# Left operands at fixed products in the pair stage and the way up, the last differences and the scan's later loads moved

## The chip, the cores and the metric

One core of one Trainium2 chip runs the whole program. The metric is device time in microseconds (us): the median of the runs of one kernel. The kernel before took 2461.01 us in the median of three runs (2454.09, 2461.01, 2461.89). The engines are TensorE (PE, the matmuls), VectorE (DVE), ScalarE (ACT), GpSimd (POOL) and SyncE (SP, which issues most DMA transfers). Each engine works through its own list of instructions in a fixed order.

## What is computed

One layer of a streaming encoder on 1088 tokens (1024 of a new stream, 64 of a running one), width 1024, all in fp32. Cut to what matters:

```
xn = rmsnorm(x);  z, xbc, dt, q, k, v, g_ssm, g_att = split(xn @ w_in)
y  = scan(silu(conv4(xbc)), softplus(dt), state)      # 32 heads in 4 groups
y  = rmsnorm(y * silu(z))
o  = attention(rope(rmsnorm(q)), rope(rmsnorm(k)) + cached keys, v)   # softmax - lam * softmax
x += (sig(g_ssm) * (y @ w_bs) + sig(g_att) * (o @ w_ba)) @ w_out
ha, hb = split(rmsnorm(x) @ w_up);  x += (silu(conv3(ha)) * hb) @ w_down
```

The outputs are the new x, the keys and values, the states of the scan and the last rows of both convolutions.

## The kernel before

**Products.** An fp32 operand is split in two parts that TensorE takes at full rate: hi, a cast by ACT, and lo, the difference from hi, made by DVE (`split`, L412). One product is then three matmuls of 128x128 by 128x272. Three stretches of the program multiply 2x2 blocks with seven block products instead of eight (a Strassen-Winograd scheme): the projections to q, k and z (16 pairs of output tiles in the list `INPUT`, called here the **pair stage**), the FFN's first matrix (22 pairs, the **way up**) and its second (12 pairs, the **way down**).

**A pair** has 7 products p0 to p6 in two halves s (columns), so 14 steps of 12 matmuls, in the order p0 s0, p0 s1, p1 s0 and so on. Step number = 2p+s. Accumulator banks and readers (`in_pair`, L574 on; the way up has the same in `pair`): p0 goes to bank a and ACT copies it to u1 (L622); p1 goes to b and DVE adds u1, giving u2 (L624); p2 goes on in a; p3 goes on in b, and DVE adds it to u1 (L626); p4 is in bank c and p5 in bank d, both read by DVE (L634); p6 goes on in bank c. So p6 of a half can't start until DVE has read p4 of that half; three steps (36 matmuls) lie between the end of p4 s0 and the start of p6 s0.

**Left operands.** Each pair has seven, built from four weight blocks q11, q12, q21, q22 that two loads `w_f` bring: q11, s2 = q21+q22-q11, q12, q11-q21, s1 = q21+q22, q22, and q12-s2. The sums are four operations on POOL (for pairs 0 and 1 on DVE), then each is split into hi and lo. Operands 0 to 3 go to four `wh` buffers, 4 to 6 to the two buffers of `w_hi` and `w_lo`. In the pair stage and on the way up a generator (`left_parts`, L495) yields the next pair's operands one by one; `more_left` (L539) takes one after each second step (s = 1), so all seven are made during the pair ahead. In the pair stage the lo part lags: `split_left` (L480) notes it and `low_left` (L488) writes it at the next call, behind DVE's last read. On the way down, the code already has a table (`down_left`, `lefts_at`): loads at step 4, operands 0 to 3 of the next pair at steps 8, 10, 11, 13, and operands 4, 5, 6 of a pair at steps 0, 1, 3 of that pair itself.

**Beside the pairs** of the pair stage runs side work, one unit per step (`take_turn`): step sizes, cached keys, and after the q and k pairs the finishing of q and k: POOL fetches a half row from the scratch `q_r` or `k_r` into a ring of four buffers `fx`, DVE scales it (L760 with the norm), ACT casts the hi part, SP stores it to `q_st` or `k_st`, DVE makes the rest (L717) and SP stores that. `done` (L601) squares a finished tile on ACT, DVE sums the squares (L614), and SP stores the tile. Rows live in two pools, `rows_l` and `rows_r`, which are opened where earlier pools (`xn`, `rr` on one side, `raw`, `st` on the other) have been released, so their first use waits for the last readers of those.

**The scan's start.** While the last attention and gate tiles run, `scan` fetches its first inputs: two spans of `in` (three loads each, L1170, L1171), three steps of `bc` (L1183), two `zin` (L1176). SP also issues the stores of the gate tiles, `g_sc<-gt` (L884), whose three `gt` buffers ACT fills from the banks (L881), and of the attention's output, `o_sc<-oh`, `o_sc<-ol` (L1103).

**The start of the way down.** It multiplies differences of rows that the way up has stored: `differences_of` (L1600 on) loads two rows `ht`, does four subtractions on DVE (L1607 to L1610) and stores to `t_sc`. A couple of rows is done at step 6 of the second pair after its last row was made; the last two couples come after pairs 1 and 2 of the way down. Right operands n and m are loaded, then split in place by L413 (ACT) and L414 (DVE).

**What sets the order.** The Tile framework schedules the program once, by a modelled timeline, priorities and the pins `issue_after` (this instruction not ahead of that one on its engine); the lists that result are fixed. So a move in the code moves neighbours too.

Of the kernel before, what the change touches and what calls it, by code (L numbers as in the profile page):

```python
# [62 lines left out]
IN_ROWS = dict(fs=2, fu=2, fp=3, fc=3, fx=4, ss=2)  # L63
# [27 lines left out]
def hybrid_layer(ctx: ExitStack, tc: tile.TileContext, xT, xt, prm, cst, rope, wvd, win, wbs, wba, wout, wup, wdn,  # L91
# [378 lines left out]
    def row(tag, name, dt=F32):  # L470
        if tag == "fa":
            return rows_l.tile([P, KT * P], dt, name=name, tag=tag, bufs=4)
        w = {"ss": T, "fs": 4 * P}.get(tag, HT)
        return rows_r.tile([P, w], dt, name=name, tag=tag, bufs=IN_ROWS[tag])

    def couple(t, n=2):
        return t[:, : n * QW].rearrange("p (a t) -> p a t", a=n)

    low, lagging = [], [True]

    def split_left(hi, lo, src):
        S.copy(hi, src)  # L482
        if lagging[0] and "read" in seen:
            low.append((hi, lo, src))
        else:
            V.tensor_tensor(out=lo, in0=src, in1=hi, op=ALU.subtract)  # L486

    def low_left():  # L488
        if low:
            with tc.issue_after(seen["read"].ins):  # L490
                for hi, lo, src in low:
                    V.tensor_tensor(out=lo, in0=src, in1=hi, op=ALU.subtract)
            low.clear()

    def left_parts(blocks, early=None, by=G, order=(0, 1, 2, 3)):  # L495
# [12 lines left out]
        def own(src):  # L508
            t = row("fa", "wh", R32)
            hi, lo = t[:, :n], t[:, 4 * P : 4 * P + n]  # L510
            split_left(hi, lo, src)
            return hi, lo

        def shared():
            t = [wp.tile([P, wide], R32, name=x, tag=x, bufs=2) for x in ("w_hi", "w_lo")]
            for i, src in enumerate((s1, q22)):
                hi, lo = (x[:, 512 * i : 512 * i + n] for x in t)
                split_left(hi, lo, src)
# [17 lines left out]
        split_left(hi, lo, s2)  # L536
        yield 6, (hi, lo)

    def more_left(f):  # L539
        low_left()  # L540
        x = next(coming, None)
        if x is not None:
            left.setdefault(f, {})[x[0]] = x[1]

# [21 lines left out]
    def split_part(n, *behind):  # L566
        with ExitStack() as pins:
            for x in behind:
                pins.enter_context(tc.issue_after(x.ins))
            for s in range(2):  # L570
                hi, lo = parts[n, s]
                split(hi, lo, lo.bitcast(F32))

    def in_pair(n):  # L574
# [43 lines left out]
        for _ in range(14):  # L618
# [8 lines left out]
            else:  # L627
# [7 lines left out]
                if s == 1:  # L635
                    done(r, c)
# [98 lines left out]
    def finishing(kind):  # L735
# [3 lines left out]
        for _ in range(4):  # L739
            yield  # L740
# [86 lines left out]
    coming = in_parts(1, early[1])  # L827
# [8 lines left out]
    for p, s in rest:  # L836
        pairs[0].send((p, s))
        if s == 1:
            more_left(1)
            if p in LATER:  # L840
                split_part(LATER[p], seen["copy"], seen["read"])
    while len(left[1]) < 7:
        more_left(1)
    beside = chain(one_by_one(steps()), cached_keys())
    for n in range(1, len(INPUT)):
        coming = in_parts(n + 1) if n + 1 < len(INPUT) else iter(())
        u = pairs[1] if n == 1 else begun_in(n)
        for at, (p, s) in enumerate(rest if n == 1 else [(p, s) for p in range(7) for s in range(2)]):
            u.send((p, s))
            if s == 1:  # L850
                more_left(n + 1)
# [4 lines left out]
        while n + 1 < len(INPUT) and len(left[n + 1]) < 7:  # L856
            more_left(n + 1)
        low_left()
        del left[n]
        if n == Q_DONE:  # L860
            beside = chain(beside, finishing("q"), finishing("k"))
    while take_turn(0):
        for _ in range(2):
            take_turn(1)
    lagging[0] = False
# [78 lines left out]
    with (tc.tile_pool(name="ak", bufs=1) as ak, tc.tile_pool(name="at", bufs=1) as at,  # L944
# [131 lines left out]
        def head_out(h, o_t, ssq, s0):  # L1076
# [15 lines left out]
            for b0 in range(0, 9, 4):  # L1092
# [9 lines left out]
                for u, t in enumerate((hi, lo)):  # L1102
                    load(out=o_sc[D * u + P * h : D * u + P * (h + 1), b0 * P : b0 * P + w], in_=t.bitcast(F32))  # L1103
# [60 lines left out]
    with (tc.tile_pool(name="sin", bufs=1) as sin, tc.tile_pool(name="sp", bufs=1) as sp,  # L1164
# [112 lines left out]
        def scan():  # L1277
            spans = [(g, c, w) for g in range(4) for c, w in WIDE]
            steps = [(i, g, c, w, o) for i, (g, c, w) in enumerate(spans) for o in range(0, w, P)]
            got, due = [fetch(*x) for x in spans[:2]], None  # L1280
            asked = [ask(*x) for x in steps[:3]]
            gates = [fetch_z(*x) for x in spans[:2]]
# [225 lines left out]

    ffn_o = tri[:, : 4 * FT].rearrange("p (f c) -> p f c", c=4)
# [144 lines left out]
    made = {}  # L1654

    def down_left(i, what):

        g, m = divmod(i, 4)
        n = P * (DOWN[g] // 2)
        if what == "load":  # L1660
            q = []
            for r in (m, m + 4):
                o = 1024 * first[g] + 2 * n * r
                w = wp.tile([P, wide], F32, name="w_f", tag="w_f", bufs=2)
                load(out=w[:, : 2 * n], in_=wdn[:, o : o + 2 * n])
                q += [w[:, :n], w[:, n : 2 * n]]
            q11, q12, q21, q22 = q
# [263 lines left out]
```

## Time and profile before

| | |
|---|---|
| median of 3 runs | 2461.01 us (2454.09 to 2461.89) |
| the profiled execution | 2447.27 us, of which the span is 2445.5 us |
| PE busy | 2394.9 us, 98% of the span, 18744 matmuls |
| DVE, ACT, POOL busy | 71%, 50%, 28% |
| granted TensorE clock | 0.995 in the mean |

The profiled execution is one run, 13.7 us under the median of the other three. Stretches by the place of the lines in the span: values 0 to 115 us, pair stage 115 to 483, attention 483 to about 1085, scan 1085 to about 1500, branches and output 1500 to 1720, way up 1720 to about 2195, way down about 2195 to 2436. A matmul's row gives about 290 ns but one starts about every 125 ns, since they overlap; a gap between matmuls is idle time of PE, and rows of waits name what ended it. Instructions of DVE also overlap a little (0.43 us each, one every 0.35).

### The profile page before, as it was taken

Reading aid. Unit: us, or ns where it says so; the run is one execution under the profiler, and the core shown is the slowest. Engines: PE = TensorE matmul, PEld = TensorE weight load, DVE = VectorE, ACT = ScalarE, POOL = GpSimd, SP = SyncE. Lnnn points to the kernel's source line nnn. Section 1 sums busy time; section 2 is a strip of 40 time slices with the busy share of each in tenths; the row PEclk is TensorE's granted clock in tenths of the full one; section 3 lists DMA queues with packets and bytes.
Section 4 is the critical chain, followed back from the end, with each engine's and each line's share of the span. In section 5 each row is a group of like instructions: output and inputs, shape, how many; then the busy total and the mean of one; then the engine's idle time right before and its main releaser. Section 6 shows DMA issues by size and latency. Waiting matters only on the chain.

```text
span 2445.5 us, 49342 instructions
## 1 busy us (share of the span) xinstructions
PE 2394.9 (98%) x18744; PEld 2319.6 (95%) x18744; DVE 1744.6 (71%) x3118; ACT 1224.1 (50%) x2707; POOL 689.0 (28%) x753
## 2 busy tenths in 40 slices
PE   8999999999999999999999999999999999999998
PEld 8999989999999999998899999999999999999998
DVE  4586867668687786865787665756977777777765
ACT  7354464356565665647665554434543343352442
POOL 0023333201011010104443331013255555534444
PEclk9999999999999999999999999999999999999999
DMA  7855758665445344345897954764123423467876
GB/s 245 283 177 184 241 184 317 219 192 154 152 151 161 123 148 134 114 154 176 270 332 257 339 176 149 218 205 150 58 90 145 154 80 142 150 212 214 220 177 105
DMA packets 283088, 449.79 MB, mean 184 GB/s; under 512 B 35609, under 2 KB 189346, under 8 KB 282850
## 3 DMA queue, kind: packets, MB, share of 16 engines
q1 hardware_dynamic: 271810, 420.30, 51.8%
q0 software_dynamic: 11040, 26.34, 5.4%
q8 instruction: 147, 2.41, 0.4%
q14 instruction: 91, 0.75, 0.1%
HBM read 294.03 MB, written 152.50 MB: 183 GB/s over the span
## 4 chain that ended last, share of the span: by engine, by line
PE 66%; DMA 7%; DVE 7%; issue 3%; POOL 2%; ACT 1%; SPq 0%; POOLq 0%; DVEq 0%; ACTq 0%
PE mx L1528 9%; PE mm L162 9%; PE mm L164 9%; PE mm L163 9%; PE mm L1528 4%; PE mx L1748 4%; PE po L1071 3%; PE mx L164 2%; PE mx L162 2%; PE mx L163 2%; PE mm L1748 2%; PE mx L587 2%; PE sc L1023 2%; PE sc L1022 2%; PE pt L1051 1%
## 5 line engine op out<-in xcount | busy, mean ns | idle before, releaser
L162 PE MATMUL mm<-b,w_hi 128*128 128x272 f32 x1792 | 529.0, 295 | 0.8 <-DVE b_g L230 0.7
L164 PE MATMUL mm<-b,w_lo 128*128 128x272 f32 x1792 | 522.7, 292 | 1.8 <-DVE w_lo L156 1.8
L163 PE MATMUL mm<-b,w_hi 128*128 128x272 f32 x1792 | 520.8, 291 | 0.0
L162 PEld LDWEIGHTS mm<-b,w_hi 128*128 128x128 f32 x1792 | 337.6, 188 | 7.3 <-issue 3.8
L163 PEld LDWEIGHTS mm<-b,w_hi 128*128 128x128 f32 x1792 | 337.8, 189 | 3.3 <-issue 2.6
L164 PEld LDWEIGHTS mm<-b,w_lo 128*128 128x128 f32 x1792 | 337.1, 188 | 3.7 <-DVE w_lo L156 2.4
L912 DVE SCALAR_TENSOR_TENSOR cc<-pre,par,cc 128x272 f32<-128x272 f32 (+1 forms) x288 | 140.1, 490 | 16.4 <-ACT cc L910 13.6
L1528 PE MATMUL mx<-m,w_hi 128*128 128x272 f32 x760 | 146.1, 289 | 1.3 <-ACT m L413 1.3
L1528 PE MATMUL mx<-n,wh 128*128 128x272 f32 x1080 | 144.3, 288 | 1.9 <-DVE u L1555 1.0
L1528 PEld LDWEIGHTS mx<-n,wh 128*128 128x128 f32 x1080 | 138.5, 188 | 2.5 <-DVE u L1555 1.2
L900 POOL COPY pre<-pre 128x3 f32<-128x3 f32 x72 | 22.4, 312 | 418.3 <-DVE cc L914 186.2
L1036 ACT ACTIVATE p_t<-sc,mx 128x512 f32<-128x512 f32 (+6 forms) x144 | 106.1, 739 | 63.4 <-DVE mx L1027 30.9
L156 DVE TENSOR_TENSOR w_lo<-w_f,w_hi 128x1024 fp32r<-128x1024 f32 (+1 forms) x82 | 103.7, 1266 | 46.2 <-ACT w_hi L155 43.5
L155 ACT CAST w_hi<-w_f 128x1024 fp32r<-128x1024 f32 (+1 forms) x82 | 85.9, 1048 | 70.2 <-PE mm L163 43.0
L1528 PEld LDWEIGHTS mx<-m,w_hi 128*128 128x128 f32 x760 | 119.3, 188 | 1.5 <-ACT m L413 1.5
L1545 POOL TENSOR_TENSOR hb<-hb,cc 128x544 f32<-128x544 f32 (+2 forms) x63 | 81.8, 1312 | 101.8 <-DVE hb L1566 50.6
L482 ACT CAST w_hi<-ws 128x512 fp32r<-128x512 f32 x76 | 46.9, 617 | 126.5 <-PE mx L1528 75.0
L1528 PE MATMUL mx<-m,w_lo 128*128 128x272 f32 x380 | 109.7, 289 | 0.0
L1208 ACT ACTIVATE bc<-bc,nacum 128x128 f32<-128x128 f32 (+1 forms) x288 | 87.2, 384 | 16.1 <-POOL bc L1206 15.7
L505 POOL TENSOR_TENSOR ws<-w_f 128x512 f32<-128x512 f32 x34 | 48.5, 1425 | 154.1 <-DMA w_f<-in_win_dram 64.7
L486 DVE TENSOR_TENSOR wh<-w_f,wh 128x512 fp32r<-128x512 f32 x65 | 66.7, 1028 | 26.9 <-ACT wh L482 26.9
L1430 POOL TENSOR_TENSOR s<-s,sq 128x272 f32<-128x272 f32 x24 | 30.5, 1271 | 192.9 <-DMA out_dram<-x 131.2
(467 smaller groups left out, 7093.2 us busy)
## 6 DMA issues: line engine op xcount, KB each, us to landing
w_f<-in_win_dram SPq DMA_DIRECT2D x78, 512.0 KB, 4.2
w_f<-in_wup_dram SPq DMA_DIRECT2D x45, 512.0 KB, 3.4
bc<-a_sc SPq DMA_DIRECT2D x32, 512.0 KB, 5.9
h_sc<-hb SPq DMA_DIRECT2D x44, 272.0 KB, 2.1
ht<-h_sc SPq DMA_DIRECT2D x22, 544.0 KB, 4.8
t_sc<-ht SPq DMA_DIRECT2D x22, 544.0 KB, 2.7
out_dram<-yq POOLq DMA_DIRECT2D x44, 272.0 KB, 5.2
x_sc<-cc SPq DMA_DIRECT2D x72, 136.0 KB, 2.4
```

What stands on the lines that cost most here:

```text
L155: S.copy(hi, w)
L156: V.tensor_tensor(out=lo, in0=w, in1=hi, op=ALU.subtract)
L162: PE.matmul(ps, a_hi, b_hi, start=i == 0, stop=False)
L163: PE.matmul(ps, a_hi, b_lo, start=False, stop=False)
L164: PE.matmul(ps, a_lo, b_hi, start=False, stop=i == n - 1)
L912: V.scalar_tensor_tensor(cc[:, :m], pre[:, i : i + m], cw(i), cc[:, :m], ALU.mult, ALU.add)
L1036: act(p_t[:n, :nk], sc[c][:n, :nk], AF.Exp, bias=mx[:n, c : c + 1], accum_out=dst)
L1071: PE.matmul(po[:n, :P], a_t[b // 4][:kw, b % 4 * P : b % 4 * P + n], rhs, start=b == 0, stop=b == nb - 1)
L1208: act(bc[:L, e, :L], bc[:L, e, :L], AF.Exp, bias=nacum[:L, ch, 8 * g + e : 8 * g + e + 1])
L1528: PE.matmul(ps, w[x][:, c], b[y][:, k], start=start and k == i == 0, stop=k == 3 and i == 2, skip_group_check=not start)
L1545: (V if f + 1 == FT else G).tensor_tensor(out=hb[h][:, o : o + n], in0=hb[h][:, o : o + n], in1=cc[:, d : d + n], op=ALU.mult)
L1748: PE.matmul(ps, w[y][:, c], b[z][:, k], start=start and k == j == 0, stop=k == n - 1 and j == 2, skip_group_check=not start)
```

## The change

- **Left operands.** The generator and the lagging lo parts go (`split_left`, `low_left`). The way down's table becomes general (`make_left`, `lefts_at`) and serves the pair stage and the way up too: loads at step 4, operands 0 to 3 of the next pair at steps 8, 10, 11, 13, operands 4, 5, 6 at steps 0, 1, 3 of the pair itself, each pinned behind the newest copy (ACT) and read (DVE). Pairs 1 and 2 of the pair stage and pair 1 of the way up, which begin with fewer steps, have tables of their own. The four sums of pair 1 of the pair stage move from DVE to POOL. The last sum is written over q12 instead of s2.
- **Rows.** The buffers `fs` (sums) and `fu` (u1, u2) move from pool `rows_r` to `rows_l`, so they lie over other earlier pools.
- **Squares and stores.** `done` is put off by one step (`ripe`), and the finishing of q and k starts one turn later (5 for 4).
- **Scan.** Only the first span and the first `bc` are loaded ahead; the second span, two `bc` and both `zin` come after the last store to `o_sc`.
- **Differences.** The third last couple moves from step 6 of the last pair of the way up to the end of pair 0 of the way down.

Line numbers after the change, for those below: L624 becomes L662, L626 L664, L634 L672, L614 L652, L760 L798, L717 L755; splits of left operands (L482, L486, L492) become L413, L414; L884 becomes L923, L1103 L1142, L1170 L1209, L1171 L1210, L1176 L1215, L1183 L1222, L1607 to L1610 L1650 to L1653, L1753, L1758, L1760, L1762 L1746, L1751, L1753, L1755.

The order of the lists shows it in three places. First DVE in the pair stage, pair 7 of the pairs (the last of k), from the second read of p1 to the reads of p4 (L634). `wh<-` and `w_lo<-` are lo parts of left operands, `x` are rows of the finishing, `ss` the sum of squares. Before:

```order
L624 TENSOR_TENSOR u_3518<-mx,u_3517 128x272 x2
L492 TENSOR_TENSOR wh<-w_f,wh 128x512
L760 SCALAR_TENSOR_TENSOR x<-x,wq_1552,ss 128x544
L717 TENSOR_TENSOR x<-x,xh 128x544
L492 TENSOR_TENSOR wh<-ws_3554,wh 128x512
L626 TENSOR_TENSOR u_3517<-mx,u_3517 128x272
L717 TENSOR_TENSOR x<-x,xh 128x544
L760 SCALAR_TENSOR_TENSOR x<-x,wq_1552,ss 128x544
L614 TENSOR_TENSOR ss<-ss,sq 128x544
L626 TENSOR_TENSOR u_3517<-mx,u_3517 128x272
L492 TENSOR_TENSOR wh<-w_f,wh 128x512
L634 TENSOR_TENSOR pre<-mx,u_3517 128x272
```

And after, the same stretch of DVE's list:

```order
L662 TENSOR_TENSOR u_3496<-mx,u_3495 128x272 x2
L414 TENSOR_TENSOR w_lo<-w_f,w_hi 128x512
L798 SCALAR_TENSOR_TENSOR x<-x,wq_1552,ss 128x544
L755 TENSOR_TENSOR x<-x,xh 128x544
L664 TENSOR_TENSOR u_3495<-mx,u_3495 128x272
L755 TENSOR_TENSOR x<-x,xh 128x544
L652 TENSOR_TENSOR ss<-ss,sq 128x544
L798 SCALAR_TENSOR_TENSOR x<-x,wq_1552,ss 128x544
L664 TENSOR_TENSOR u_3495<-mx,u_3495 128x272
L672 TENSOR_TENSOR pre<-mx,u_3495 128x272
L414 TENSOR_TENSOR wh<-w_f,wh 128x512
```

Of three lo parts between the reads of p1 and the first read of p4, one is left; one now stands behind that read. Second, SP at the start of the scan, before:

```order
L1170 DMA in<-x_sc 128x384 x2
L1171 DMA in<-x_sc 128x4x384
L1170 DMA in<-x_sc 128x384 x2
L1171 DMA in<-x_sc 128x4x384
L1183 DMA bc<-a_sc 128x1024 x3
L1176 DMA zin<-z_sc 128x4x384 x2
L1183 DMA bc<-a_sc 128x1024
L884 DMA g_sc<-gt 128x272
L1103 DMA o_sc<-oh 128x512
```

After, in SP's list:

```order
L1209 DMA in<-x_sc 128x384 x2
L1210 DMA in<-x_sc 128x4x384
L1222 DMA bc<-a_sc 128x1024
L923 DMA g_sc<-gt 128x272 x2
L1142 DMA o_sc<-oh 128x512
L1142 DMA o_sc<-ol 128x512
L1142 DMA o_sc<-oh 128x512
L1142 DMA o_sc<-ol 128x512
L923 DMA g_sc<-gt 128x272
L1142 DMA o_sc<-oh 128x64
L154 DMA w_f<-in_win_dram 128x1024
L1142 DMA o_sc<-ol 128x64
```

The stores of gates stood behind twelve loads and now stand behind four; the other loads follow behind the last row shown. Third, DVE in the first pairs of the way down, before (`yq` are outputs of the way down, L1607 is the first subtraction of a couple):

```order
L1545 TENSOR_TENSOR hb<-hb,cc 128x64
L1753 TENSOR_TENSOR u<-mm,u 128x272
L1607 TENSOR_TENSOR ht<-ht 128x544
L414 TENSOR_TENSOR wh<-w_f,wh 128x512
L414 TENSOR_TENSOR m_27509<-m_27509,m_27508 128x1088
L1760 TENSOR_TENSOR yq<-mx,u 128x272
```

And after, from the same read (now L1746) on:

```order
L1746 TENSOR_TENSOR u<-mm,u 128x272
L414 TENSOR_TENSOR wh<-w_f,wh 128x512
L1753 TENSOR_TENSOR yq<-mx,u 128x272
L1755 TENSOR_TENSOR u<-mx,u 128x272
L414 TENSOR_TENSOR m_27454<-m_27454,m_27453 128x1088
L414 TENSOR_TENSOR m_27499<-m_27499,m_27498 128x1088
```

The subtraction L1607 is gone from between the read and the splits, and the read p4 (L1753) now stands ahead of the splits of m.

The diff, cut to its core (the removed code of the way down's own table equals the new functions but for names):

```diff
 RAW = 6
-IN_ROWS = dict(fs=2, fu=2, fp=3, fc=3, fx=4, ss=2)
+IN_ROWS = dict(fa=4, fs=2, fu=2, fp=3, fc=3, fx=4, ss=2)
 ZS = 4
...
-        if tag == "fa":
-            return rows_l.tile([P, KT * P], dt, name=name, tag=tag, bufs=4)
-        w = {"ss": T, "fs": 4 * P}.get(tag, HT)
+        if tag in ("fa", "fs", "fu"):
+            w = {"fa": KT * P, "fs": 4 * P, "fu": HT}[tag]
+            return rows_l.tile([P, w], dt, name=name, tag=tag, bufs=IN_ROWS[tag])
+        w = {"ss": T}.get(tag, HT)
         return rows_r.tile([P, w], dt, name=name, tag=tag, bufs=IN_ROWS[tag])
...
-    low, lagging = [], [True]
-
-    def split_left(hi, lo, src):
-        S.copy(hi, src)
-        if lagging[0] and "read" in seen:
-            low.append((hi, lo, src))
-        else:
-            V.tensor_tensor(out=lo, in0=src, in1=hi, op=ALU.subtract)
-
-    def low_left():
-        if low:
-            with tc.issue_after(seen["read"].ins):
-                for hi, lo, src in low:
-                    V.tensor_tensor(out=lo, in0=src, in1=hi, op=ALU.subtract)
-            low.clear()
...
-        low_left()
         x = next(coming, None)
...
+    def make_left(x, what, blocks):
+
+        if what == "load":
+            q = []
+            for src in blocks:
+                w = wp.tile([P, wide], F32, name="w_f", tag="w_f", bufs=2)
+                n = src.shape[1] // 2
+                load(out=w[:, : 2 * n], in_=src)
+                q += [w[:, :n], w[:, n : 2 * n]]
+            q11, q12, q21, q22 = q
+            s1, s2 = (row("fs", y)[:, :n] for y in ("ws1", "ws2"))
+            G.tensor_tensor(out=s1, in0=q21, in1=q22, op=ALU.add)
+            G.tensor_tensor(out=s2, in0=s1, in1=q11, op=ALU.subtract)
+            G.tensor_tensor(out=q21, in0=q11, in1=q21, op=ALU.subtract)
+            made[x] = [q11, s2, q12, q21, s1, q22, q12]
+            left.setdefault(x, {})
+            return
+        src = made[x][what]
+        n = src.shape[1]
+        if what < 4:
+            t = row("fa", "wh", R32)
+            hi, lo = t[:, :n], t[:, 4 * P : 4 * P + n]
+        elif what == 6:
+            hi, lo = (wp.tile([P, wide], R32, name=y, tag=y, bufs=2)[:, :n] for y in ("w_hi", "w_lo"))
+        else:
+            if len(made[x]) == 7:
+                made[x].append([wp.tile([P, wide], R32, name=y, tag=y, bufs=2) for y in ("w_hi", "w_lo")])
+            hi, lo = (t[:, 512 * (what - 4) : 512 * (what - 4) + n] for t in made[x][7])
+        if what == 3:
+            G.tensor_tensor(out=made[x][6], in0=made[x][6], in1=made[x][1], op=ALU.subtract)
+        with after("copy", "read"):
+            split(hi, lo, src)
+        left[x][what] = hi, lo
+
+    def lefts_at(x, at, blocks, token_major=lambda x: False, short=None):
+
+        todo = []
+        if x in made:
+            todo += {0: [(x, 6)]}.get(at, []) if token_major(x) else {0: [(x, 4)], 1: [(x, 5)], 3: [(x, 6)]}.get(at, [])
+        y = x + 1
+        if blocks:
+            mine = {1: "load", 8: 0, 9: 1, 11: 2, 12: 3} if token_major(x) else {4: "load", 8: 0, 10: 1, 11: 2, 13: 3}
+            mine = short or mine
+            if at in mine:
+                todo.append((y, mine[at]))
+            if token_major(y):
+                todo += {13: [(y, 5), (y, 4)]}.get(at, []) if token_major(x) else {12: [(y, 5)], 13: [(y, 4)]}.get(at, [])
+        for y, what in todo:
+            make_left(y, what, blocks)
...
+    ripe = []
 
     def in_pair(n):
...
-                    done(r, c)
+                    ripe.append(lambda r=r, c=c: done(r, c))
...
-        for _ in range(4):
+        for _ in range(5):
...
-    for p, s in rest:
+    for at, (p, s) in enumerate(rest):
         pairs[0].send((p, s))
-        if s == 1:
-            more_left(1)
-            if p in LATER:
-                split_part(LATER[p], seen["copy"], seen["read"])
-    while len(left[1]) < 7:
-        more_left(1)
+        while ripe:
+            ripe.pop(0)()
+        if at in (0, 5, 7):
+            make_left(1, {0: "load", 5: 1, 7: 3}[at], blocks_of(1))
+        if s == 1 and p in LATER:
+            split_part(LATER[p], seen["copy"], seen["read"])
...
-        coming = in_parts(n + 1) if n + 1 < len(INPUT) else iter(())
+        blocks = blocks_of(n + 1) if n + 1 < len(INPUT) else None
         u = pairs[1] if n == 1 else begun_in(n)
         for at, (p, s) in enumerate(rest if n == 1 else [(p, s) for p in range(7) for s in range(2)]):
+            old, ripe = ripe, []
             u.send((p, s))
-            if s == 1:
-                more_left(n + 1)
+            for x in old:
+                x()
+            lefts_at(n, at, blocks, short={3: "load", 7: 0, 9: 1} if n == 1 else None)
+            if n == 2 and at in (0, 1):
+                make_left(2, 2 + at, blocks)
             take_turn(at)
...
-                    load(out=o_sc[D * u + P * h : D * u + P * (h + 1), b0 * P : b0 * P + w], in_=t.bitcast(F32))
+                    seen["out"] = load(out=o_sc[D * u + P * h : D * u + P * (h + 1), b0 * P : b0 * P + w], in_=t.bitcast(F32))
...
-            got, due = [fetch(*x) for x in spans[:2]], None
-            asked = [ask(*x) for x in steps[:3]]
-            gates = [fetch_z(*x) for x in spans[:2]]
+            got, due = [fetch(*spans[0])], None
+            asked = [ask(*steps[0])]
+            with tc.issue_after(seen["out"].ins):
+                asked += [ask(*x) for x in steps[1:3]]
+                got.append(fetch(*spans[1]))
+                gates = [fetch_z(*x) for x in spans[:2]]
...
-        coming = up_parts(f + 1) if f + 1 < FT else iter(())
+        blocks = [wup[f + 1 + r * FT] for r in range(2)] if f + 1 < FT else down_blocks(0)
...
-            if f + 1 == FT:
-                lefts_at(-1, at)
-            elif s == 1:
-                more_left(f + 1)
+            lefts_at(f, at, blocks, token_major, {0: "load", 4: 0, 6: 1, 7: 2, 9: 3} if f == 1 else None)
...
-                    if i + n + 2 == f:
+                    if i + n + 2 == f and f + 1 < FT:
...
-        if i in (1, 2):
+        if i in (0, 1, 2):
```

76 lines of the change are left out of this document (14 added, 62 removed).

## The prediction

> **What bounds the kernel now.** The page first: who is busy, and with what.
>
> ```profile
> span 2445.5 us, 49342 instructions
> PE 2394.9 (98%) x18744; PEld 2319.6 (95%) x18744; DVE 1744.6 (71%) x3118; ACT 1224.1 (50%) x2707; POOL 689.0 (28%) x753
> ```
>
> TensorE is the bound, and the change takes no matmul away (the lists of both kernels hold the same products). So nothing can be gained but PE's idle time: 2445.5 − 2394.9 = 50.6 us, 2.1% of the span. Where it lies, the view by stretches tells (start and end of the stretch, its length, then busy us of PE, PEld, DVE, ACT, POOL, the granted clock, the DMA share and GB/s):
>
> ```profile
> 115.00:130.00 15.00, 12.65 (x101) 12.43 (x100) 7.24 (x13) 6.67 (x15) 1.30 (x2) 1.00 0.99 322
> 130.00:170.00 40.00, 38.22 (x297) 37.34 (x297) 39.46 (x65) 20.98 (x35) 6.80 (x6) 1.00 0.47 163
> 170.00:483.00 313.00, 302.57 (x2333) 297.13 (x2333) 231.19 (x389) 150.31 (x273) 100.55 (x96) 0.99 0.66 224
> 1085.00:1200.00 115.00, 108.93 (x859) 98.07 (x858) 71.09 (x87) 71.93 (x180) 41.85 (x28) 0.97 0.64 214
> 1760.00:2195.00 435.00, 433.26 (x3439) 432.10 (x3437) 322.50 (x489) 175.66 (x316) 227.17 (x247) 1.00 0.38 134
> 2195.00:2220.00 25.00, 19.92 (x131) 18.07 (x132) 25.00 (x36) 12.39 (x18) 8.43 (x5) 0.91 0.80 258
> 2220.00:2436.00 216.00, 215.49 (x1704) 214.76 (x1703) 145.66 (x238) 79.99 (x146) 94.04 (x89) 0.99 0.76 181
> ```
>
> Idle is length less PE busy: 2.35, 1.78 and 10.43 us in the pair stage, 6.07 at the scan's start, 1.74 in the way up (but for its first 40 us), 5.08 in the first 25 us of the way down, 0.51 in all that follows. All that the change touches thus holds some 27 us. The last row is the one to remember: the way down already makes its left operands at fixed products, and PE idles 0.51 of 216 us there. What ended the waits, the view of PE's waits tells (us in total, times, longest):
>
> ```profile
> PE mm L587 <- DVE pre L634: 6.2, 5, 2.8
> PE mx L587 <- DVE pre L634: 5.2, 4, 1.7
> PE mx L162 <- ACT gt L881: 3.9, 1, 3.9
> PE mx L587 <- ACT u L622: 2.3, 1, 2.3
> PE mm L1748 <- ACT yq L1755: 2.2, 2, 1.8
> PE mx L1748 <- DVE m L414: 1.7, 2, 1.1
> PE mm L1528 <- DVE hb L1564: 1.7, 2, 1.1
> ```
>
> The first two are one thing: p6 waits for DVE's read of p4, nine times, 11.4 us. It is the largest wait of the stretches that the change touches.
>
> **Part 1, left operands in the pair stage.** One of these nine, in the timeline of DVE (start, duration, line; in brackets idle time before it and what ended that) and one row each of POOL and PE:
>
> ```profile
> 285.00 1.28 DVE L760 SCALAR_TENSOR_TENSOR x<-x,wq,ss 128x544 f32<-128x544 f32 x1 [3.10 <-DMA x<-q_r]
> 286.20 1.81 DVE L717 TENSOR_TENSOR x<-x,xh 128x544 fp32r<-128x544 f32 x1
> 288.12 1.60 DVE L492 TENSOR_TENSOR wh<-ws,wh 128x512 fp32r<-128x512 f32 x1
> 289.64 0.43 DVE L626 TENSOR_TENSOR u<-mx,u 128x272 f32<-128x272 f32 x1
> 289.99 1.68 DVE L717 TENSOR_TENSOR x<-x,xh 128x544 fp32r<-128x544 f32 x1
> 291.60 0.77 DVE L760 SCALAR_TENSOR_TENSOR x<-x,wq,ss 128x544 f32<-128x544 f32 x1
> 292.29 0.71 DVE L614 TENSOR_TENSOR ss<-ss,sq 128x544 f32<-128x544 f32 x1
> 293.28 0.68 DVE L492 TENSOR_TENSOR wh<-w_f,wh 128x512 fp32r<-128x512 f32 x1
> 293.88 0.43 DVE L634 TENSOR_TENSOR pre<-mx,u 128x272 f32<-128x272 f32 x1
> ```
>
> ```profile
> 285.77 1.66 POOL L506 TENSOR_TENSOR ws<-ws,w_f 128x512 f32<-128x512 f32 x1
> ```
>
> ```profile
> 294.36 0.52 PE L587 MATMUL mx<-b,w_hi 128*128 128x272 f32 x2 [1.53 <-DVE pre L634]
> ```
>
> DVE loses 3.10 us to a fetch of the finishing (`x<-q_r`), then works off what has queued up, slowed beside POOL's sums, and reads p4 at 293.88, 1.53 us too late. Between the fetch and that read stand two lo parts: the one at 288.12 holds DVE until 289.64 (1.52 us), the one at 293.28 until 293.88 (0.60). The order after has neither there: one lo part comes ahead of the fetch's first user, one behind the read. The read comes 1.52 + 0.60 = 2.1 us earlier, so this wait of 1.53 goes. With plain lo parts (0.60 each, the row at 293.28) it would come 1.2 earlier. Nine waits at 1.2 to 2.1 would all but vanish (11.4 / 9 = 1.27 each). But the fetch is as late as before, and the longest wait is 2.8; and what is moved has to run somewhere: two lo parts per pair now stand between the reads of p4, p5 and p6. I take 8 of the 11.4, with ends 0 (the fetch alone decides) and 11.4. Late next is the read of p4 s1, behind one lo part.
>
> What is neutral: the same number of splits; ACT's casts are half idle time (150 of 313 us busy). `w_f` must be loaded at step 4 instead of in two goes; it lands after 4.2 us in the median, and operand 1, due at step 10, needs two sums (1.66 us in the row of POOL): 7.5 us, in six steps of 1.5 us (12 matmuls at 302.57 / 2333 = 0.13). If operand 0 is late, ACT's cast waits and with it p0's copy to u1. `done` one step later costs nothing: its squares are used only in the finishing.
>
> ```profile
> w_f<-in_win_dram SPq DMA_DIRECT2D x78, 512.0 KB, 4.2
> g_sc<-gt SPq DMA_DIRECT2D x64, 136.0 KB, 3.2
> ```
>
> The four sums of pair 1 leave DVE, which is busy 39.46 of 40 us from 130 to 170: at 0.69 each (the row below) 2.8 us less for it there, on POOL (6.80 of 40 busy) they have room. [...]
>
> **Part 2, rows u1 in other memory.** The first copy of the pair stage:
>
> ```profile
> 123.36 1.25 ACT L622 COPY u<-mx 128x272 f32<-128x272 f32 x4 [7.04 <-DMA out_dram<-vo]
> ```
>
> ```profile
> 123.79 0.69 DVE L505 TENSOR_TENSOR ws<-w_f 128x512 f32<-128x512 f32 x1 [7.18 <-ACT u L622]
> ```
>
> ACT idled 7.04 us with the product ready, and PE stopped 2.3 us for it: the memory of u1 was that of pools whose last reader is a store. In the new pool it lies over `xn` and `rr`, which hold operands of the stretch ahead: PE's first waiting products are done, and DVE has stood still since 123.79 − 7.18 = 116.6, so no reader is left by then. The wait goes, and DVE, whose first sum waited for the same memory, begins up to 7 us earlier. What is late next are DVE's splits in the 40 us after, with 1.78 us of idle PE. I take −2.5: ends 0 and −(2.35 + 1.78) = −4.1.
>
> **Part 3, the scan's loads.** SP's issues and ACT's next free buffer:
>
> ```profile
> 1082.04 0.86 SPq L1170 DMA_DIRECT2D in<-x_sc  x2
> ...
> 1092.60 0.72 SPq L884 DMA_DIRECT2D g_sc<-gt  x1
> ```
>
> ```profile
> 1103.70 0.39 ACT L881 COPY gt<-mx 128x272 f32<-128x272 f32 x1 [11.69 <-DMA g_sc<-gt]
> ```
>
> Twelve loads hold SP for 10.6 us, the store of a gate is issued at 1092.60 and its buffer is free at 1103.70, 11.1 us later where the median is 3.2. PE stops 3.9 us for it. After the change four loads stand ahead. With a third of the loads the issue comes some 7 us sooner; the crowd then falls on the stores that follow and on `bc`, which ACT needs in its own order. I take −2.5, with ends −3.9 (nothing takes its place) and +3.9 (it stops as long again at the first steps of the scan). [...]
>
> **Part 4, way up.** Its idle is 1.74 us of 435; 1.7 us in two waits (p6 for p4's read, L1564). Operands move as in part 1, and at most these go; the new places may bring as many. Zero, ends −1.7 and +3.
>
> **Part 5, the last differences.** DVE's list at the way down's start:
>
> ```profile
> 2198.53 0.71 DVE L1610 TENSOR_TENSOR ht<-ht 128x544 f32<-128x544 f32 x1
> ...
> 2212.46 1.47 DVE L1607 TENSOR_TENSOR ht<-ht 128x544 f32<-128x544 f32 x1
> 2213.85 1.75 DVE L414 TENSOR_TENSOR wh<-w_f,wh 128x512 fp32r<-128x512 f32 x1
> 2215.52 2.36 DVE L414 TENSOR_TENSOR m<-m,m 128x1088 fp32r<-128x1088 f32 x1
> ```
>
> DVE is busy 25.00 of 25 us there. A couple's four subtractions (0.71 each) and the first of the next (1.47) leave that stretch, about 4 us of queue, and one subtraction stays: some 3 us less ahead of the last split of m, which ends the waits for m (1.7 us); the waits for ACT (2.2) follow from casts, not from DVE. I take −2.5 of the idle 5.08: ends −5.1 and +1, since the couple now comes in pair 0's end, where the way down runs nearly full.
>
> **The sum.** −8 − 2.5 − 2.5 + 0 − 2.5 = −15.5 us. The profiled execution took 2447.27 us (span 2445.5 and 1.8 around it), which would become 2431.8. The median of the runs is 13.7 us above the profiled one, so the same change gives 2461.0 − 15.5 = 2445.5. I predict 2445.5 for the median. Best ends: −11.4 − 4.1 − 3.9 − 1.7 − 5.1 = −26.2, 2434.8. About 0.3% (7.4 us) can be told from no change: the three runs differ by as much.
>
> **Rivals.**
> A, the fetch decides. DVE's 3.10 us wait for `x<-q_r` stays, and the lo parts that are moved only make the later reads late. For it: the fetch ring of four isn't touched by the change, and the finishing even starts a turn later. Against it: the order shows two lo parts fewer in front of the read. Then part 1 gives 0: −7.5, 2453.5, at the edge of the 0.3%.
> B, slower: POOL's sums (loads at step 4, so from about step 7 on) run into the reads of p4 in every pair. Price: beside the sums four operations of pair 7 took 0.51 + 1.10 + 0.92 + 0.97 = 3.5 us more (1.28, 1.81, 1.60, 1.68 against 0.77, 0.71, 0.68, 0.71 of equal shape in the same rows). If p6 then waits 1.8 us in each of 15 pairs, that is 27 us in place of 11.4, less 7.5 of the other parts: +8, 2469. It decides from (11.4 + 7.5) / 15 = 1.3 us a pair. Against it: in pair 7 of before the sums lay in the same steps (285 to 291), and the way down, with the same table, has 0.51 us of idle time; but no finishing runs beside that.
> C, nothing: the waits only change their names, since PE's list was built for the old order; within 0.3%.
>
> **Chances.** The forecast 0.64, A 0.17 (0.07 of it beyond 0.3%), B 0.14, C 0.05. Faster 0.71, same 0.15, slower 0.14. The range: down to 2433 (the best ends, and 2 us of the runs' scatter), up to 2464, which takes in A and C and leaves the most of B out.
>
> **What would show it.** Right: no wait of 2 us at the first L660 copy; the waits of L625 on L672 under 4 us in sum; no idle time of over 5 us on ACT at the gates, and PE's stop at 1104 gone; the first 25 us of the way down with under 3 us idle. Wrong: waits of L625 on L672 in nearly every pair, or new ones on ACT's casts for w_f (B); a stop of PE for bc or y at 1105 to 1120; p6 of the way up waiting in the pairs that load `ht`.

## The result and the profile after

The kernel after took 2446.01 us in the median of five runs (2445.18 to 2447.92), the kernel before 2459.14 us beside it (2452.98 to 2461.89). The ratio is 0.9954, 95% interval 0.9936 to 0.9971: faster by some 11 to 13 us. The forecast was 2445.5, in a range of 2433 to 2464. So the sum came out, and by luck: its terms, as the experiments show, did not.

The page of the kernel after, its first two lines:

```profile
span 2444.2 us, 49255 instructions
PE 2391.9 (98%) x18744; PEld 2319.4 (95%) x18744; DVE 1736.7 (71%) x3114; ACT 1221.6 (50%) x2707; POOL 707.2 (29%) x757
```

The span is only 1.3 us shorter than the one the prediction was read from, 2445.5. That profiled execution of before (2447.27 us) was quicker than any timed run of before in this study. One profile is one draw, and a comparison of these two alone says nearly nothing about the 13 us.

The kernel after by stretches (columns as in the prediction):

```profile
115.00:130.00 15.00, 13.57 (x110) 13.34 (x108) 9.67 (x16) 7.03 (x18) 1.31 (x2) 1.00 0.90 288
130.00:170.00 40.00, 35.32 (x265) 34.61 (x263) 35.52 (x58) 18.00 (x29) 10.73 (x8) 0.96 0.50 174
170.00:483.00 313.00, 302.11 (x2346) 297.60 (x2345) 235.12 (x388) 152.73 (x279) 108.38 (x99) 0.99 0.66 224
1085.00:1200.00 115.00, 109.18 (x880) 98.07 (x880) 77.93 (x98) 77.07 (x197) 45.40 (x31) 1.00 0.71 237
1760.00:2195.00 435.00, 435.00 (x3462) 434.86 (x3461) 313.60 (x491) 175.05 (x317) 234.77 (x248) 1.00 0.37 133
2195.00:2220.00 25.00, 22.89 (x176) 22.02 (x175) 23.09 (x35) 12.58 (x19) 9.03 (x7) 1.00 0.63 181
2220.00:2436.00 216.00, 210.02 (x1647) 208.31 (x1646) 148.35 (x239) 78.16 (x143) 94.02 (x88) 0.99 0.79 192
```

From 1760 to 2195 the way up has no idle time left (1.74 us before), the first 25 us of the way down have 2.11 (5.08 before), but the rest of the way down has 5.98 (0.51 before), and 130 to 170 has 4.68 (1.78 before). The scan's first 115 us have 5.82 (6.07 before), now at a granted clock of 1.00 for 0.97. PE's waits in the stretches that the change touches, the longest:

```profile
PE mx L625 <- DVE pre L672: 6.1, 3, 3.2
PE mx L625 <- ACT wh L413: 3.6, 1, 3.6
PE yi L1256 <- DVE y L1264: 3.1, 1, 3.1
PE mx L1741 <- DVE yq L1753: 2.2, 1, 2.2
PE tr L1235 <- DMA in<-x_sc: 2.2, 2, 1.8
PE mx L625 <- DVE u L662: 1.8, 2, 1.1
PE mx L1741 <- DVE n L414: 1.7, 1, 1.7
PE mm L625 <- DVE pre L672: 1.6, 1, 1.6
PE mx L625 <- ACT u L660: 1.4, 1, 1.4
```

The waits of p6 for p4 fell from nine (11.4 us) to four (7.7), yet a wait of 3.6 for a left operand and others stand beside them. At the scan the 3.9 us at the gates are gone; waits of 1.8 and 3.1 have come.

### The profile page after: what moved, and what is told of

It is laid out like the page before. It is cut to its first block, busy times and chain, and to the rows that moved or that the text cites. A ratio compares the mean times of both kernels' runs of the same rounds, so it can differ in the third digit from the quotient of the medians.

```text
span 2444.2 us, 49255 instructions
## 1 busy us (share of the span) xinstructions
PE 2391.9 (98%) x18744; PEld 2319.4 (95%) x18744; DVE 1736.7 (71%) x3114; ACT 1221.6 (50%) x2707; POOL 707.2 (29%) x757
## 4 chain that ended last, share of the span: by engine, by line
PE 77%; DMA 8%; DVE 7%; issue 3%; ACT 2%; POOL 1%; SPq 1%; POOLq 0%; DVEq 0%; ACTq 0%
PE mx L1571 13%; PE mm L162 9%; PE mm L164 9%; PE mm L163 9%; PE mm L1571 5%; PE mx L625 4%; PE mx L1741 3%; PE po L1110 3%; PE mx L164 3%; PE mx L162 3%; PE mx L163 3%; PE mm L625 2%; PE sc L1061 2%; PE sc L1062 2%; PE pt L1090 1%
## 5 line engine op out<-in xcount | busy, mean ns | idle before, releaser
L414 DVE TENSOR_TENSOR wh<-w_f,wh 128x512 fp32r<-128x512 f32 (+1 forms) x144 | 128.5, 893 | 1.6 <-ACT wh L413 1.6
L542 POOL TENSOR_TENSOR ws<-w_f 128x512 f32<-128x512 f32 (+1 forms) x47 | 63.2, 1345 | 204.2 <-DMA w_f<-in_win_dram 93.5
L413 ACT CAST wh<-w_f 128x512 fp32r<-128x512 f32 (+1 forms) x144 | 86.9, 611 | 62.3 <-DMA w_f<-in_win_dram 20.8
L1582 DVE SCALAR_TENSOR_TENSOR cc<-pre,par,cc 128x544 f32<-128x544 f32 (+1 forms) x88 | 96.6, 1099 | 6.5 <-ACT cc L1580 5.2
L1588 POOL TENSOR_TENSOR hb<-hb,cc 128x544 f32<-128x544 f32 (+2 forms) x63 | 72.8, 1170 | 77.7 <-issue 42.8
```

What stands on the lines that cost most here:

```text
L1582: V.scalar_tensor_tensor(cc[:, :n], pre[h][:, i : i + n], cw(i), cc[:, :n], ALU.mult, ALU.add)
```

## What a stop of TensorE costs

The prediction priced a stop at its length. The views of stretches show that this is too little. One stop each, with ten us before it and after it; first a second profile of the kernel before, then the kernel after (the granted clock is the third column from the end):

```profile
505.70:515.70 10.00, 7.21 (x56) 6.90 (x54) 2.43 (x5) 2.16 (x5) 0.00 (x0) 1.00 0.86 251
515.70:522.50 6.80, 6.12 (x25) 6.12 (x26) 5.58 (x13) 4.57 (x14) 0.00 (x0) 0.50 0.44 135
522.50:532.50 10.00, 10.00 (x80) 9.88 (x80) 6.01 (x15) 5.36 (x18) 0.68 (x4) 1.00 0.58 188
```

```profile
138.50:148.50 10.00, 6.26 (x45) 5.82 (x46) 10.00 (x11) 3.78 (x5) 5.62 (x3) 1.00 0.21 83
148.50:151.90 3.40, 3.40 (x17) 3.40 (x16) 3.40 (x6) 2.31 (x4) 1.70 (x2) 0.50 0.21 82
151.90:161.90 10.00, 10.00 (x81) 10.00 (x81) 8.31 (x19) 1.96 (x4) 0.12 (x1) 1.00 0.31 110
```

Behind a stop of 3.5 us at 512 to 516 the granted clock is 0.50 for 6.8 us, behind the one at 143 to 147 for 3.4 us. By that column the half clock gives away 3.4 and 1.7 us on top of the stop; in the kernel after a matmul of 128x272 started every 0.227 us from 148.5 to 151.9, and every 0.126 in the ten us behind. In the 14 profiles of this study (the last 10 us left out) it comes in pieces of 3.41 or 6.83 us, but for one of 40.96 us at a stop of 31 us in the run with side work every fourth step. Counted over all other stops behind the first 12 us (a piece that begins from 1 us before to 4.5 us after the stop's end; lengths here go from the start of one matmul to the start of the next, about 0.3 us more than the idle time in a row), stops of 3 us and more went with it in 26 of 33 cases, stops of 2 to 3 us in 24 of 49, stops of 0.7 to 2 us in 14 of 308. So a stop of 3 us costs about 5 and three of 1 us cost 3, an estimate from these counts and pieces. What sets the length of a piece, and which of the shorter stops bring one, the runs do not show.

## The experiments

Parts are undone in the kernel after, or done alone in the kernel before. In the run with the way up alone, whose code is the kernel after with all other parts undone, the traces list the same instructions in the same order as before on every engine up to 1757 us, where the way up has begun. Each set ran with runs of before on the same chip. "To before" is the ratio with its interval; between two sets it is the fairer comparison, since the runs of before differ from set to set.

| kernel | median us | before beside it | to before |
|---|---|---|---|
| after | 2446.0 | 2459.1 | 0.9954 [0.9936, 0.9971] |
| before, again | 2456.1 | 2459.3 | 0.9983 [0.9971, 0.9995] |
| after, pair stage's lefts undone | 2445.2 | 2459.3 | 0.9948 [0.9933, 0.9962] |
| after, scan undone | 2448.5 | 2459.3 | 0.9963 [0.9949, 0.9976] |
| after, rows undone | 2451.9 | 2459.3 | 0.9970 [0.9953, 0.9987] |
| after, way up undone | 2458.8 | 2458.9 | 0.9997 [0.9987, 1.0007] |
| after, differences undone | 2449.8 | 2458.9 | 0.9957 [0.9941, 0.9972] |
| after, side work every 4th step | 2486.7 | 2458.9 | 1.0112 [1.0092, 1.0131] |
| after, pair stage and differences undone | 2446.3 | 2458.9 | 0.9947 [0.9932, 0.9963] |
| after, way up and differences undone | 2449.0 | 2457.6 | 0.9967 [0.9957, 0.9978] |
| before with way up alone | 2456.1 | 2457.6 | 0.9996 [0.9986, 1.0007] |
| before with rows alone | 2456.4 | 2457.6 | 0.9997 [0.9984, 1.0010] |
| before with rows and scan | 2452.9 | 2458.0 | 0.9981 [0.9970, 0.9993] |

Of the kernels with one part undone, only the one without the way up has an interval that does not overlap that of the kernel after.

And each profile's stretches, in us, worked out from the start of the first matmul of a stretch to that of the next (pair stage and way up to their last matmul; scan from there being its first to its last transpose, `tr`; the attention and the output, which the change does not touch, are the stretches between). The last column is way up and way down together.

| profile | pair stage | attention | scan | way up | way down | both |
|---|---|---|---|---|---|---|
| before | 367.6 | 606.3 | 382.0 | 477.2 | 238.7 | 715.9 |
| before, again | 370.7 | 612.3 | 384.2 | 479.6 | 238.5 | 718.1 |
| after | 369.3 | 606.6 | 378.2 | 474.3 | 240.0 | 714.4 |
| pair stage undone | 368.8 | 605.9 | 377.9 | 473.1 | 242.6 | 715.6 |
| scan undone | 371.0 | 606.7 | 380.3 | 473.1 | 244.9 | 718.0 |
| rows undone | 371.2 | 607.5 | 377.4 | 473.1 | 241.5 | 714.6 |
| way up undone | 369.5 | 607.4 | 376.0 | 477.3 | 246.7 | 724.0 |
| differences undone | 370.1 | 606.4 | 377.8 | 474.8 | 241.6 | 716.4 |
| side work every 4th step | 365.0 | 647.6 | 378.1 | 473.3 | 243.1 | 716.4 |
| pair stage and differences undone | 373.4 | 607.0 | 378.4 | 474.4 | 242.2 | 716.6 |
| way up and differences undone | 367.8 | 608.1 | 378.8 | 480.4 | 238.5 | 719.0 |
| before with way up | 370.6 | 611.0 | 383.0 | 475.3 | 243.0 | 718.3 |
| before with rows | 369.5 | 606.9 | 382.0 | 477.8 | 239.1 | 716.9 |
| before with rows and scan | 370.1 | 608.3 | 378.0 | 479.7 | 238.8 | 718.4 |

**The kernel before, once more.** No edit.

> The kernel before, unchanged, for a second profiled execution and five more timed runs. Its first profiled execution took 2447.3 us, its runs 2453 to 2462, while five runs of the kernel after lie between 2445.2 and 2447.9. Theory P (the prediction's: the nine waits of p6 for the read of p4 and the stop at the scan's start are there in every run): ratio 1.000, the second profile shows the same waits in the pair stage within 3 us (11.4 us there). Rival S (the kernel before differs from run to run in one stage, and the first profile is of a lucky run): a profile of 2453 to 2462 whose one stage is 6 to 15 us longer than in the first.

Twelve runs, 2449.6 to 2461.3, ratio 0.9983. Two samples of the same code thus differ by 0.17%, with an interval that leaves out 1: differences of 4 us between kernels are not told apart here, whatever the interval says. Its profile has a span of 2459.6. The waits of p6 sum to 12.4 (6.2 in five, 6.2 in six), as P has it. The 14 us over the first profile are not of one stage, as S had it, but of several, the largest in the attention (+6.0), which the change doesn't touch:

```profile
516.38 0.69 PE L1022 MATMUL sc<-kh,q 128*128 128x384 f32 x1 [3.48 <-ACT p_t L1036]
```

```profile
ACT w_hi L155 <- DMA w_f<-in_win_dram: 7.3, 1, 7.3
```

There ACT stood 7.3 us for a weight load with its softmax behind it, PE stood 3.5 us, and the half clock of the stretch 515.7 to 522.5 above followed.

**Left operands of the pair stage undone.** The generator, the lagging lo parts, `done` at once and four turns, as before:

```diff
-                    ripe.append(lambda r=r, c=c: done(r, c))
+                    done(r, c)
...
-            lefts_at(n, at, blocks, short={3: "load", 7: 0, 9: 1} if n == 1 else None)
+            if s == 1:
+                more_left(n + 1)
```

> The kernel after with the left operands of the pair stage as before (generator, lagging lo parts, done at once, finishing after 4 turns); rows, scan, way up and differences stay changed. Theory P: 8 us of the gain are lost, ratio to the kernel before 0.998 (gain about 5 to 7 us), and the waits of p6 for p4 in the pair stage come to about 11 us. Rival A (the fetch decides those waits, so the pair stage gives nothing): as fast as the kernel after, 0.9945 to 0.996.

As fast as the kernel after (2445.2). In its profile, the waits of p6 (these are rows of its pair stage) are back:

```profile
PE mx L642 <- DVE pre L689: 5.6, 6, 2.8
PE mm L642 <- DVE pre L689: 5.1, 3, 2.8
PE mx L642 <- DVE t L414: 2.2, 1, 2.2
```

10.7 us in nine waits, and yet the stage takes 368.8 us against 369.3. P falls on the time: the part takes away waits of p6 and brings others as long (their sums stand with part 1 below).

**Scan undone.** The added lines:

```diff
+            got, due = [fetch(*x) for x in spans[:2]], None
+            asked = [ask(*x) for x in steps[:3]]
+            gates = [fetch_z(*x) for x in spans[:2]]
```

> The kernel after with the scan's loads as before (two spans, three bc, two zin ahead of the stores). Theory P: 2.5 us slower than the kernel after, ratio to before about 0.9965; PE stops about 4 us at the gates near 1104 us. Rival C (the stop only changes its place): as fast as the kernel after, within 1 us.

2448.5, 2.5 slower than after, as P had it, though no more than the scatter. The stop is back (ACT, waiting for a store of a gate):

```profile
1106.72 0.39 ACT L920 COPY gt<-mx 128x272 f32<-128x272 f32 x1 [10.87 <-DMA g_sc<-gt]
```

In the table the five profiles with the old loads have 380.3 to 384.2 us of scan, the nine with the new 376.0 to 378.8, with no overlap. That is the surest gain of all parts: means 382.3 and 377.8, 4.5 us. Part of it lies in where the stretch begins: attention and scan together, without the profiles with a stop of 3 us and more in the attention, take 988.1 us with the old loads (three) and 985.0 with the new (eight), 3.1 us less.

**Rows undone, and rows alone.**

```diff
-        if tag in ("fa", "fs", "fu"):
+        if tag == "fa":
```

> The kernel after with the buffers of sums and of u1, u2 back in the right-hand pool. Theory P: the 2.3 us stop at the first copy of the pair stage is back, 2.5 us slower than the kernel after, ratio about 0.9965. Rival: DVE's splits in the 40 us after take its place in both kernels, so no difference over 1 us.

> The kernel before with the buffers of sums and u1, u2 in the left-hand pool, nothing else. Prediction: 2.5 us faster, ratio 0.999, the 2.6 to 3.2 us stop at the first copy of the pair stage gone. Undoing the same in the kernel after cost 5.9 us in the median: if that holds here too, ratio 0.9976. Rival: DVE's splits take its place and nothing is gained, ratio 1.000.

Undone in the kernel after it costs 5.9 us by the medians (seven runs, 2445.3 to 2460.4) and 3.9 by the ratios, whose intervals overlap; done alone in the kernel before it gives 1.3 (0.9997). The stop at the first copy is 2.3, 2.9, 3.3 and 3.4 us (idle time) in four profiles with the old pool, and at most 1.4 in the others. But with the new pool there are waits for splits at 135 to 143 (1.0 to 2.2 us), and the pair stage is no shorter. Whether the 5.9 us are the part's is left open by 1.3.

**Way up undone, differences undone, both, and the way up alone.**

```diff
-            lefts_at(f, at, blocks, token_major, {0: "load", 4: 0, 6: 1, 7: 2, 9: 3} if f == 1 else None)
+            if f + 1 == FT:
+                lefts_at(f, at, down_blocks(0), token_major)
+            elif s == 1:
+                more_left(f + 1)
...
```

```diff
-                    if i + n + 2 == f and f + 1 < FT:
+                    if i + n + 2 == f:
...
-        if i in (0, 1, 2):
+        if i in (1, 2):
```

> The kernel after with the left operands of the way up as before (generator after each second step). The prediction put this part at zero, ends -1.7 and +3. In the profiles, though, the way up took 477.2 and 479.6 us in the two of before and 474.3, 473.1, 473.1, 473.1 us in the four with the new table. Prediction: as fast as the kernel after, within 1 us. Theory U (the table of the way up carries a gain, since its waits of p6 for p4 are gone): 3 to 5 us slower than the kernel after, ratio to before 0.997, and the way up at 477 us or more.

2458.8: with the old way up under it, the rest of the change gives nothing. U seemed to hold, and more.

> The kernel after with the third last couple of differences back in the last pair of the way up. Prediction: 2.5 us slower. Theory D (the move brings a new wait: at 2236 us PE waits 2.25 us because DVE stood 3.42 us for the rows ht, so the term has the wrong sign): as fast or up to 2 us faster than the kernel after, way up and way down together 714 us or less, no stop of over 2 us at 2236.

2449.8, 3.8 us slower than after by the medians of two sets, but only 0.7 by the ratios (0.9957 and 0.9954). So neither the prediction's 2.5 nor D's gain can be told apart here. The stop of over 2 us at 2236 is gone from that profile, as D said; way up and way down together take 716.4 us, not D's 714 or less.

> The kernel after with both the left operands of the way up and the differences as before; pair stage, rows and scan stay changed. With the way up alone undone the kernel was 12.8 us slower than after, but its profile shows new stops of 3.4 and 1.9 us in the way down, where the moved differences wait for ht. Theory U (the way up's table itself carries the 12.8 us): about 2458 us, ratio to before 0.999 to 1.000. Theory I (the table saves 3 to 5 us in the way up, and the rest of the 12.8 came from the moved differences meeting another order): about 2449 to 2451 us, ratio 0.996 to 0.997.

2449.0: with the differences undone as well, 10 us are back (7 by the ratios). U falls, I holds.

> The kernel before with the new table of left operands on the way up alone. Theory U: 11 to 13 us faster than before, ratio about 0.995. Theory I: 3 to 5 us faster, ratio 0.998 to 0.9988, and the way up at 474 us against 477 to 480 us. Prediction: no difference.

2456.1, ratio 0.9996, way up 475.3: U falls again; I's 3 to 5 us do not show in the time.

Read together: the new table shortens the way up from 478.7 (mean of six profiles) to 473.9 (eight), where the prediction had zero; but the way down behind it is longer, 242.4 (the same eight) against 238.7 (the five with neither table nor moved differences), so both together gain about 2 us (715.8 in the five profiles with table and moved differences, 717.7 in the five with neither). The moved differences are not what lengthens the way down: with the table it takes 242.3 us in the three profiles without them and 242.4 in the five with them. Only the old way up with moved differences is bad, 724.0. There DVE stands for the rows `ht` of the moved couple and PE for DVE:

```profile
2252.42 0.72 DVE L1650 TENSOR_TENSOR ht<-ht 128x544 f32<-128x544 f32 x1 [2.87 <-DMA ht<-h_sc]
2256.82 0.73 DVE L1651 TENSOR_TENSOR ht<-ht 128x544 f32<-128x544 f32 x1 [2.72 <-DMA ht<-h_sc]
```

```profile
2254.16 3.09 PE L1741 MATMUL mm<-n,wh 128*128 128x272 f32 x12 [3.14 <-DVE u L1746]
```

One profile shows it, and it accounts for 8 of the 12.8 us (10.6 by the ratios). The same wait stands in the kernel after, with one stop of PE of 2.2 us behind it (the row of waits for yq above):

```profile
2234.38 0.72 DVE L1651 TENSOR_TENSOR ht<-ht 128x544 f32<-128x544 f32 x1 [3.42 <-DMA ht<-h_sc]
```

**Side work every fourth step.**

```diff
-        if at % 3 == 0:
+        if at % 4 == 0:
             new = next(beside, False)
```

> The kernel after with a new unit of side work in the pair stage at every fourth step instead of every third, so that the ring of four buffers of the finishing has a third more time. Rival A (the fetch decides: POOL waits for a store to free a buffer, DVE for the fetch, p6 for DVE): the waits of p6 for p4 fall under 3 us in sum, and the pair stage gets 4 to 8 us shorter than the 369 us it took in the profile after. Theory P (DVE's queue of lo parts decides): no change, 368 to 371 us. If the finishing no longer fits beside the pairs, a tail of it would make the stage longer.

2486.7. The pair stage shrank to 365.0, 4.3 less than after, as A had it, but the waits of p6 still sum to 7.1, and the finishing no longer fitted: the attention waited for its last stores.

```profile
PE sc L1061 <- DMA out_dram<-x: 30.9, 1, 30.9
```

So A is half borne out. DVE's waits for a fetch are gone from the stage (6.2 us in the kernel after), yet the waits of p6 hardly fell (7.1 us for 7.7): the longest, 4.2 us, stands behind 3.1 us in which DVE waited for a store of the finishing. And less side work ran in the stage at all, since its tail came behind it. So it is not shown that the ring of the fetch is worth the 4.3 us.

**Rows and scan alone, and the change without the pair stage and the differences.**

> The kernel before with two parts of the change only: the buffers of sums and u1, u2 in the left-hand pool, and the scan's later loads behind the last stores. All left operands and the differences are as before. Theory M (memory and DMA order carry the gain, the tables of left operands in the pair stage nothing): as fast as the kernel with pair stage, rows and scan changed, which took 2449.0 us, so 2448 to 2451, ratio 0.9965 to 0.997, the scan stretch at 376 to 379 us. Theory L (the pair stage's table carries part of it): 2453 us or more, ratio 0.998, since rows alone gave 1.3 us and the scan's stretch is shorter by 4 to 5 us in the profiles.

2452.9, L's number: with the pair stage's table the same kernel took 2449.0. But the intervals of the two (0.9970 to 0.9993, 0.9957 to 0.9978) overlap, the pair stage takes 370.1 and 367.8 us in the two profiles, and the same table gave nothing in the full kernel. It is not settled.

> The kernel after without the two parts that seem to give nothing: left operands of the pair stage and differences as before; rows, scan and way up as after. If the parts add up (left operands of the pair stage 0 to 1 us worse than before, differences 0 to 2 us worse): 1 to 3 us faster than the kernel after, ratio to before 0.994. By the prediction it would be 10 us slower than the kernel after.

2446.3, neither faster nor slower than after: the parts left out give nothing beside the others. No kernel here clearly beat the kernel after.

## Why the prediction came out, and where its steps failed

- **The total**: 2445.5 forecast, 2446.0 measured; faster by more than 0.3%, as the likeliest case had it.
- **Part 1, −8 us, failed.** The step "the read comes 2.1 us earlier, so this wait goes" holds for single waits (nine became four), but the mean of the pair stage is 369.8 us in the six profiles with the table and 370.1 in the seven without it (side work at every fourth step left out). Two things stand against the 8 us. The waits of p6 for p4 fell by 3.4 us only, from 11.4 in the mean of the seven to 8.0 in the mean of the six. And what the part named and costed at nothing, a late operand, came in each of the six (3.6 us, once 2.4), while none of the seven waits over 0.3 us there. The operand, number 1 of pair 1 (counted from 0, the pair whose sums moved to POOL):

```profile
146.49 0.62 ACT L413 CAST wh<-ws 128x512 fp32r<-128x512 f32 x1 [4.82 <-POOL ws L543]
```

```profile
129.02 1.44 SPq L538 DMA_DIRECT2D w_f<-in_win_dram  x1
...
131.05 1.17 SPq L538 DMA_DIRECT2D w_f<-in_win_dram  x1
```

```profile
142.81 1.38 POOL L542 TENSOR_TENSOR ws<-w_f 128x512 f32<-128x512 f32 x1 [13.36 <-DMA w_f<-in_win_dram]
```

SP issued the two loads of `w_f` at 129.0 and 131.1, behind four loads of right operands, and POOL could begin its sums at 142.8 only, 11.8 us after the second, where the prediction took the median of 4.2: a median of the whole program was used where DMA is at its fullest (99% in the row 115 to 130 of before). The prediction also gave the operand six steps from its loads, as in the general table; pair 1 has a table of its own with five, in which its 7.5 us just fit (5 steps of 1.5 us) and 11.8 us for the loads alone do not. The longest of the waits of p6 that are left is rival A's, in the kernel after at 408 to 417: POOL waits for a store to free a buffer, DVE for the fetch, PE for DVE:

```profile
411.47 0.54 POOL L794 DMA_DIRECT2D x<-k_r  x1 [4.34 <-DMA k_st<-x]
```

```profile
413.49 1.47 DVE L798 SCALAR_TENSOR_TENSOR x<-x,par,ss 128x544 f32<-128x544 f32 x1 [3.60 <-DMA x<-k_r]
```

```profile
417.08 0.52 PE L625 MATMUL mx<-b,w_hi 128*128 128x272 f32 x2 [3.23 <-DVE pre L672]
```

- **Part 2, −2.5.** The stop at the first copy went or shrank; what is late next was named (DVE's splits) and took it back in the stage. In time between 1.3 and 5.9 us: open.
- **Part 3, −2.5, right in sign and as idle time, too small by the half clock**: 4.5 us in the scan (3.1 with the attention taken in). The stop of 3.9 and the half clock that came with it (0.50 from 1102.9 to 1109.7 in the profile of before) went; 1.8 and 3.1 us came at the first steps, as the upper end allowed. In the means of the profiles PE's idle time in the scan fell from 7.1 to 4.7 us, about the 2.5 of the forecast, and what half clock gives away there fell from 2.7 to 0.8, which the prediction did not price. What is left of the scan without these two is 372.0 to 372.9 us in all 14 profiles, so nothing else is needed for its gain.
- **Part 4, zero, failed by the stretch**: −4.7 in the way up, outside its ends; of this the way down gave back most. "The new places may bring as many" was false in the way up itself: no wait of p6 is left there. Which new wait of the way down belongs to the table was not followed up.
- **Part 5, −2.5**: the start of the way down lost 3.0 us of idle time as said, but the moved couple brought the stop of 2.2 us for yq, which the end of +1 didn't allow for, and the rest of the way down got 5.5 us more idle time. Most of that comes with the new table of the way up, since the way down is as long without the moved couple (242.3 us). In time the part is not told from nothing: by the medians 3.8 us in the kernel after, 1.1 with the pair stage's part undone too; by the ratios 0.7 and −0.2.
- **What the sum left out**: the half clock behind each long stop, and the scatter. Taking the 15.5 from the median rather than from the first profile was what made it right: that profile had none of the attention's stop. That the terms, of which the largest gave nothing, still come within half a us of the median is luck.
- Rival B did not come: no wait of p6 in every pair.

What is not shown is where in the timed runs the 13 us lie. The scan's gain is there in every profile (4.5 us in the mean). The rest is 2 us in the way up and down, and stops that come in some executions and not in others, such as the attention's (in two of the 14 profiles, both with the old pool and the old loads of the scan).

## What to carry to other kernels

Price a stop of TensorE by its length and by the clock behind it: by the counts above, breaking a stop of three us into shorter ones is worth more than hunting the short ones, though no run here tries it. Where a scheduler sets the order, undo each part of a change in the new kernel as well as doing it alone in the old one, for the two numbers may differ by the whole gain. And look at a second profile of the same kernel before a wait is called its cost.

## What was not expected of the hardware

Half clock behind stops of only 2 to 2.5 us (15 of 31), and pieces of half clock that are 3.41 or 6.83 us long, but for one of 40.96. And the scatter of one program's runs: the timed runs of before, over all sets, lie from 2449.1 to 2468.6 us. The kernel after was run five times only (2445.2 to 2447.9), which says little of its own scatter.
